# Moving the buffers of a three-layer block within the on-chip memory: weights and residual to the high end, matmul operands and stage pools to the low end

## The chip, the cores and the metric

The kernel runs on one core of a Trainium2 chip, as one launch. The time is the device time of that launch in microseconds, and the median of the runs is what counts. TensorE (PE in the profile) multiplies; its weight loads are shown apart (PEld). VectorE is DVE, ScalarE is ACT, GpSimd is POOL, and SP is SyncE, from whose queue nearly all transfers are issued. All tiles named here lie in SBUF, the on-chip memory, across its 128 partitions; an address below is the byte at which a tile starts in each partition.

## The reference

Three layers over 512 tokens of 1024 features, in float32 (`D_MODEL` 1024, feed-forward width 2816):

```python
# layer 1
attn = dilated_attention(q, k, v)                 # 8 heads, three dilations
sgu = spatial_gating(u, z, ...)                   # gated by a 128 x 128 causal mix
mixed = concat(rmsnorm(attn), rmsnorm(sgu)) @ w_out
h = h + rmsnorm(mixed)
g, up = split(rmsnorm(h) @ w_gate_up)             # 2 x 2816 columns
h = h + rmsnorm((silu(g) * up) @ w_down)
h = h + sigmoid(h @ w_pe_gate + b) * (p @ w_pe_proj)
# layers 2 and 3, each with shift, scale and gate from c
m = stick_breaking_attention(h, w_in, w_out)      # layer 2: 16 heads
m = dsa_attention(h, ...)                         # layer 3: 16 heads, 128 keys of each query picked by an index
h = h + gate * m
u = causal_conv3(rms_norm(h) @ ffn_w_up); h = h + gate * ((silu(u1) * u2) @ ffn_w_down)
```

## The kernel before, in words

Activations lie feature-major, as tiles of 128 features by 512 tokens. Every weight product is made in three passes of `mm3` (L104), since both operands are split into a high and a low part of type fp32r: low weights times high operand, high times high, high times low. One pass is one matmul with a stationary operand of 128 x 128 (or fewer columns) and a moving operand of 128 x 512; the page calls it `out<-moving,stationary` or the other way round, and each has its own weight load.

- **Weights.** `unit` (L87) and `units` (L110) load 128 x 1024 float32 into one of four tiles `raw` by SP's queue, ACT casts each half to `whi` (L98 or L122), and DVE takes the difference as `wlo` (L99 or L123); there are seven of each. As a rule these are the stationary operands. In the token-major products (`tok_steps`, L153) they are the moving ones.
- **Moving operands.** `hh0` to `hh7` and `hl0` to `hl7` hold the high and low parts of a layer's normed input; the up-projections of all feed-forwards read them. `Hh0` to `Hh21` and `Hl0` to `Hl21` hold the 22 feature tiles of a feed-forward's middle, which the down-projections read (`down`, L744). The attention stages' output projections read `mh`, `ml`, `k` or `q` tiles.
- **Stages.** `mixer_a` and `ffn_a` (layer 1), `mixer_sb` and `ffn_conv` (layer 2), `mixer_dsa` and `ffn_conv` (layer 3) follow each other. Each opens a pool of its own and closes it at its end, so that the next stage's pool takes the same addresses. In the feed-forwards PE has one long list of weight products. In the attention stages `attend` (L523) weaves score blocks, transposes and value products with weight products.
- **Placement.** A pool is a stack of tiles in the order of their first use, each start rounded up to a multiple of 32 bytes. Five pools that live throughout (L273 to L276 in `build`, and the residual `X0` to `X7` inside the pool `x`) lie at the bottom, in this order: constants, weights, `x`, small tiles. The stage's pool comes above them.

The starts of the tiles that matmuls read, and what is left when the start is divided by 256, as the built programs have them:

| tile | start before | by 256 | start after | by 256 |
|---|---|---|---|---|
| `raw` (4 tiles of 4096 bytes) | 22784 | 0 | 173920 | 96 |
| `whi`, `wlo` (14 of 2048) | 39168 | 0 | 190304 | 96 |
| `X0` to `X7` | 71936 | 0 | 157536 | 96 |
| `hh`, `hl` (16 of 2048) | 88320 | 0 | 16512 | 128 |
| `Hh`, `Hl` of `ffn_a` | 137888 | 160 | 49280 | 128 |
| `Hh`, `Hl` of `ffn_conv` | 154976 | 96 | 65664 | 128 |
| `mh`, `ml` of `mixer_a` | 137888 | 160 | 57472 | 128 |
| `mh` of `mixer_sb` | 158912 | 192 | 74400 | 160 |
| `q8` to `q15` of `mixer_dsa` | 129696 | 160 | 51328 | 128 |
| `q5`, `q6`, `q7` of `mixer_dsa` | 200704 | 0 | 120288 | 224 |
| `AT`, `v0` of the index in `mixer_dsa` | 162464, 146080 | 160 | 82048, 65664 | 128 |

Tiles of one row follow each other in steps of a multiple of 256, so that a row has one remainder.

Of the kernel before, what the change touches and what calls it, by code (L numbers as in the profile page):

```python
# [8 lines left out]
F32 = mybir.dt.float32  # L9
F32R = mybir.dt.float32r  # L10
# [5 lines left out]
P = 128  # L16
# [14 lines left out]
# Columns of the per-feature constants, eight (or n) columns of 128 features each.  # L31
# [25 lines left out]
class K:  # L57
# [29 lines left out]
    def unit(self, src, widths=(512, 512), eng=None):  # L87
        """One load of consecutive columns, in parts of `widths`: [(hi, lo)]."""
        nc = self.nc
        n, raw = sum(widths), src  # L90
        if src is not self.first:
            raw = self.t(self.wp, [P, UNIT], F32, "raw", bufs=4)
            nc.sync.dma_start(raw[:, :n], src[:, :n])
        out, c = [], 0
        for w in widths:
            hi = self.t(self.wp, [P, 512], F32R, "whi", bufs=7)
            lo = self.t(self.wp, [P, 512], F32R, "wlo", bufs=7)
            nc.scalar.copy(hi[:, :w], raw[:, c:c + w])  # L98
            (eng or nc.vector).tensor_sub(lo[:, :w], raw[:, c:c + w], hi[:, :w].bitcast(F32))  # L99
            out.append((hi, lo))  # L100
            c += w
        return out
# [7 lines left out]
    def units(self, srcs):  # L110
        """Two-part units of several slabs, the first parts of all before the second ones."""
# [15 lines left out]
    def slabs(self, pss, parts, xs, m=P, per=4, ks=None, n=None):  # L127
        """pss[i][m, 512] += sum over k of w_i[k].T @ x[k], k-tile by k-tile for all i together.

        parts[i]: (hi, lo) of `per` k-tiles each, in the order of xs; ks: the k-tiles of this call, of n."""  # L130
# [3 lines left out]
    def slab_steps(self, pss, parts, xs, m=P, per=4, ks=None, n=None):  # L134
        """The products of slabs() one by one, with a pause between two."""
# [12 lines left out]
    def tokmajor(self, pss, srcs, xs):  # L148
        """pss[tb][128 tokens, 512] = x.T @ w, w in units of two k-tiles."""
# [36 lines left out]
    def add_square(self, acc, src, pool=None, tag="acc", eng=None):  # L186
        """acc + src^2; returns the tile that holds the sum."""
# [10 lines left out]
    def rsqrt(self, x, tag="rc", bufs=3, scale=1.0, pool=None):  # L198
        """scale * x^-0.5 of a few columns: a seed from the exponent's bits, then Newton's steps to full precision."""
# [16 lines left out]
    def stats(self, src, ones, out=None):  # L216
        """(mean of squares + eps)^-0.5 as columns [128 tokens, 4] and along the free dimension."""
# [29 lines left out]
    def split(self, src, i, kind="h", pool=None):  # L247
        """The two parts of a moving operand, for k-tile i."""
# [7 lines left out]
    def split_scaled(self, src, col, i, kind="h", pool=None):  # L256
        """Parts of src * col (per feature)."""
# [12 lines left out]
    def build(self):  # L270
        tc, nc, a = self.tc, self.nc, self.a
        with ExitStack() as ctx:
            cp = ctx.enter_context(tc.tile_pool(name="const", bufs=1))  # L273
            self.wp = ctx.enter_context(tc.tile_pool(name="w", bufs=1))
            self.xp = ctx.enter_context(tc.tile_pool(name="x", bufs=1))
            self.sp = ctx.enter_context(tc.tile_pool(name="small", bufs=1))  # L276
# [4 lines left out]
            X = [self.t(self.xp, [P, S], F32, f"X{k}") for k in range(KD)]  # L281
            self.consts = self.t(cp, [P, NCOLS], F32, "consts")
            # what the first products need comes first
# [22 lines left out]
            # modulation: 48 columns a layer; the scales and the deferred shifts of the four norms  # L306
# [28 lines left out]
    # first block: dilated attention and spatial gating  # L335
    def mixer_a(self, X, raw):
# [9 lines left out]
        with ExitStack() as ctx:  # L346
# [4 lines left out]
            # gating: z token-major  # L351
# [12 lines left out]
            # values token-major  # L364
# [29 lines left out]
            # b_c * sum_j w[i, j] + b_s[i], for every channel and row  # L394
# [12 lines left out]
            # u feature-major, the gate and its squares  # L407
# [21 lines left out]
            # attention, by pairs of heads  # L429
# [42 lines left out]
            def filler():  # L472
# [10 lines left out]
                # output projection of the gate's part, with its norm behind it  # L483
# [14 lines left out]
            # then the attention's  # L498
# [24 lines left out]
    def attend(self, pairs, block, av, filler, budget, ahead=0):  # L523
        """Pairs of heads in two stages: the blocks of the next pair's weights, woven with a pair's values and other work.

        block(h, qb): weights of a block of queries; av(i, A): (transposes(kb), products(kb), end());
        filler: other work in steps, budget[i + 1] of them in stage i."""
# [26 lines left out]
    # pairs of 64-dim heads: a head's query parts over each other, against its key's parts twice over each other  # L554
# [26 lines left out]
    def stacked(self, ps, q, k, h, qb, stop=True):  # L581
        """Scores of a block of queries; the first block takes 256 keys, the fewest at full rate."""
# [4 lines left out]
    def post(self, X, M, R, k):  # L587
        """x + the normed branch (its gain is in M)."""
# [3 lines left out]
    def dilated_bias(self, pool, keep):  # L592
        """-(bias + log of how many branches see the pair) without the slope's part, and the distance; 1e30 where none does.

        Column u of row p is at distance d = p + 384 - u; a branch of dilation r sees d when r
        divides it and d <= 128 r (for r = 4 and 16 every d here)."""
# [5 lines left out]
        # d <= 128  # L602
        nc.vector.tensor_scalar(cnt, dist, 128.0, None, op0=ALU.is_le)
        for r in (4, 16):
            # p mod r against u mod r
# [7 lines left out]
        # counts 0..3 to -log(count), 1e30 for none  # L613
# [6 lines left out]
        # beyond the diagonal: none  # L620
# [4 lines left out]
    def softmax(self, pool, sb, nm, L, sign):  # L625
        """exp(sign * sb + nm) / its sum, rows of L."""
        nc = self.nc
        e = self.t(pool, [P, L], F32, f"A{L}", bufs=4)
# [7 lines left out]
    def av(self, pool, A, V, copy):  # L636
        """[2 x 64 dims, 512 queries] of a pair of heads: sum over key blocks of V[kb].T @ A.T, in two steps a key block.

        A[h][qb] is [queries, keys]; V(kb, h) [keys, 64]."""
# [22 lines left out]
    # gated feed-forward, then the per-layer embedding's gate  # L662
    def ffn_a(self, X, M, R):
        tc, nc, a = self.tc, self.nc, self.a
        acc, xs = None, []
        with tc.tile_pool(name="ffn", bufs=1) as fp:
# [11 lines left out]
            for n in range(KF):  # L678
# [7 lines left out]
                g = self.t(fp, [P, S], F32, "g", bufs=2)  # L686
                nc.vector.tensor_mul(g, pg, R)
                nc.scalar.activation(g, g, AF.Silu)
                u = self.t(fp, [P, S], F32, "u", bufs=2)
# [3 lines left out]
            # the embedding's operands  # L693
            es = []
            for k in range(2):
                e = self.t(self.sp, [P, S], F32, "sq", bufs=2)
                nc.scalar.dma_start(e, a["p"][:, k])
                hi = self.t(fp, [P, S], F32R, "g", bufs=2)
                lo = self.t(fp, [P, S], F32R, "u", bufs=2)
# [31 lines left out]
            for n in range(8):  # L731
# [5 lines left out]
                g = self.t(fp, [P, S], F32, "g", bufs=2)  # L737
# [12 lines left out]
    # modulation: silu(c) @ ada_w + ada_b, features on partitions, 128 a step  # L750
# [9 lines left out]
    def dots(self, jobs):  # L760
        """Rows of weights (128 outputs a job) times a row, each loaded a step ahead of its arithmetic."""
# [8 lines left out]
    def ada_steps(self, l):  # L770
# [10 lines left out]
        # all but the gate of the feed-forward, which comes last  # L781
        yield from columns(0, 40)
        for j, norm in enumerate(("norm_mix", "norm_ffn")):
            cn = COLS[f"{norm}{l}"]
            # (scale + 1) * norm
# [4 lines left out]
        # shift @ w for the four slabs that start before their norm is known  # L790
# [16 lines left out]
    def finish(self, X, n, b):  # L807
        """The next norm's operands of feature tile n: its squares, and its parts with the scale but no norm."""
# [11 lines left out]
    def enter(self, X, b, ws):  # L820
        """Four slabs whose norm and shift come behind them, then the normed operand for the others.

        Returns a function that gives slab i in a tile, and the operand."""
# [34 lines left out]
    def project(self, X, src, ms, l, gate, b):  # L858
        """x += gate * (m @ w): (start, rest), the first slabs k-tile by k-tile as their operands come."""
# [10 lines left out]
        def early():  # L870
            # as far as the last but one operand, a fourth slab too
# [19 lines left out]
    # stick-breaking attention  # L891
    def mixer_sb(self, X):
        tc, nc, a = self.tc, self.nc, self.a
        with tc.tile_pool(name="sb", bufs=1) as mp:
# [4 lines left out]
            dmask = self.t(mp, [P, S], F32, "keep", bufs=2)[:, :P]  # L899
            nc.vector.memset(dmask, 0.0)  # L900
            # key >= query: none
# [26 lines left out]
            def block(h, qb):  # L928
# [4 lines left out]
                keep = self.t(mp, [P, S], F32, "keep", bufs=2)  # L933
                nc.scalar.activation(keep[:, :L], ps[:, :L], AF.Sigmoid, scale=-1.0)
                beta = self.t(mp, [P, L], F32, f"A{L}", bufs=4)
                nc.scalar.activation(beta, ps[:, :L], AF.Sigmoid)
                # what is left of the stick before each key, from the query backwards
                # (the last key of a row is never before its query: no weight)
# [5 lines left out]
            def av(i, A):  # L944
                o, tr, mul = self.av(mp, A, lambda kb, h: V[kb][:, (2 * i + h) * 64:(2 * i + h + 1) * 64], None if i == 7 else nc.vector.tensor_copy)
# [30 lines left out]
    # feed-forward with a causal convolution over the tokens  # L976
    def ffn_conv(self, X, l):
        tc, nc, a = self.tc, self.nc, self.a
        with tc.tile_pool(name="ffn", bufs=1) as fp:
            w = a["ffn_w_up"][l]  # L980
            cc = self.t(fp, [P, 4, 44], F32, "conv")
# [4 lines left out]
            for n in range(KF):  # L986
                ys = []
                for j in range(2):
# [7 lines left out]
                    y = self.t(fp, [P, S], F32, "gu"[j], bufs=2)  # L996
# [15 lines left out]
    # sparse attention over the keys that an index picks  # L1012
    def mixer_dsa(self, X):
        tc, nc, a = self.tc, self.nc, self.a
        with ExitStack() as ctx:
            Tw = self.Tw
            mp = ctx.enter_context(tc.tile_pool(name="dsa", bufs=1))
            w = a["dsa_w_in"]
            slab, operand = self.enter(X, 2, [w[i] for i in range(4)])

            # the latent, and the index's queries
# [14 lines left out]
            # index scores and the keys they pick  # L1036
# [24 lines left out]
            def index(qb, h):  # L1061
# [13 lines left out]
                if h == IH - 1:  # L1075
                    # beyond the diagonal: the reference's floor
# [4 lines left out]
            def rounds(n):  # L1081
                # the largest of each row leave it, eight a round, equal ones by lowest index
# [12 lines left out]
            # queries, four heads at a time with their norms  # L1095
# [11 lines left out]
            def norms(h, n=4):  # L1107
                # norms of n heads up to h
# [15 lines left out]
                # the factor of the scores, its negative, and its inverse  # L1124
# [9 lines left out]
            def ahead():  # L1134
                norm = iter(())
                for h in range(5):
# [8 lines left out]
                    if h == 3:  # L1145
                        # the keys: the latent normed, with both gains
# [7 lines left out]
                # values of every head, token-major  # L1154
# [219 lines left out]
```

## Time and profile before

| | |
|---|---|
| median of 3 runs | 1977.55 us (1975.62 to 1977.94) |
| profiled execution, first to last instruction | 1975.4 us, 2.2 us under the median |
| PE busy | 97% of the span, 8610 matmuls |
| DVE, ACT, POOL busy | 67%, 46%, 21% |
| mean granted TensorE clock | 0.986 |

Matmuls overlap: a row's duration is longer than the distance from its start to the next start. What a product costs is that distance, so a run of n products is read as its length divided by n.

### The profile page before, as it was taken

How to read it: one execution, taken by the hardware profiler on the slowest of the kernel's cores; microseconds unless marked ns; L12 is line 12 of the kernel's file. 1: busy time of each engine (PE TensorE's matmuls, PEld its weight loads, DVE VectorE, ACT ScalarE, POOL GpSimd, SP SyncE). 2: the span in 40 equal slices, each digit the busy share in tenths (PEclk: the TensorE clock that was granted, in tenths of full speed). 3: DMA queues.
4: the chain of work that ended last, by engine and by line, in shares of the span. 5: the costliest groups of instructions: out<-in, count | busy, mean ns of one | idle time of the engine just before them, and what ended most of it. 6: DMA issues, size and time to landing. Idle time of an engine off the chain costs nothing.

```text
span 1975.4 us, 24114 instructions
## 1 busy us (share of the span) xinstructions
PE 1918.6 (97%) x8610; PEld 1507.0 (76%) x8610; DVE 1328.2 (67%) x2358; ACT 903.1 (46%) x1672; POOL 416.3 (21%) x376
## 2 busy tenths in 40 slices
PE   7999899999999999999999999999999999999999
PEld 5887678888887777767788888877656678888887
DVE  6686776656355966776988875568967678666421
ACT  4465443323334455554544443336588646444321
POOL 3010421111010402332212110033454241111000
PEclk8999899999999999999999999999999999999999
DMA  5232155555462432222265545522212023223331
GB/s 179 86 91 72 61 186 190 187 183 176 159 213 85 149 117 86 75 65 77 86 213 195 191 154 182 174 81 96 81 59 65 33 77 128 97 95 102 96 106 49
DMA packets 70382, 236.93 MB, mean 120 GB/s; under 512 B 8085, under 2 KB 8677, under 8 KB 70262
## 3 DMA queue, kind: packets, MB, share of 16 engines
q1 hardware_dynamic: 69556, 234.47, 35.6%
q8 instruction: 67, 1.10, 0.2%
q10 hardware_dynamic: 578, 0.85, 0.1%
q14 instruction: 53, 0.43, 0.1%
q0 software_dynamic: 128, 0.08, 0.0%
HBM read 226.87 MB, written 2.21 MB: 116 GB/s over the span
## 4 chain that ended last, share of the span: by engine, by line
PE 84%; DVE 10%; issue 3%; ACT 1%; POOL 1%; DMA 1%; ACTq 0%; DVEq 0%; POOLq 0%; SPq 0%
PE mm L81 50%; PE sc L81 27%; PE po L81 4%; PE tt L84 2%; PE tt L81 1%; DVE isc L1093 1%; DVE m L1092 1%; DVE hl L852 1%; DVE hl L262 1%; DVE wlo L123 1%; DVE wlo L99 1%; DVE Hh L850 1%; DVE X L590 0%; DVE q L850 0%; POOL acc L190 0%
## 5 line engine op out<-in xcount | busy, mean ns | idle before, releaser
L99 DVE TENSOR_TENSOR wlo<-raw,whi 128x512 fp32r<-128x512 f32 (+1 forms) x518 | 392.5, 763 | 241.2 <-ACT whi L98 236.4
L98 ACT CAST whi<-raw 128x512 fp32r<-128x512 f32 (+1 forms) x550 | 328.1, 607 | 424.4 <-PE mm L81 248.9
L81 PE MATMUL mm<-hh,wlo 128*128 128x512 f32 (+1 forms) x1000 | 407.9, 408 | 10.1 <-ACT hh L261 3.5
L81 PE MATMUL mm<-hl,whi 128*128 128x512 f32 x1032 | 402.5, 393 | 0.0
L81 PE MATMUL mm<-hh,whi 128*128 128x512 f32 (+1 forms) x1000 | 392.8, 393 | 0.0
L81 PEld LDWEIGHTS mm<-hh,wlo 128*128 128x128 f32 (+1 forms) x1000 | 189.1, 189 | 78.3 <-issue 30.3
L81 PEld LDWEIGHTS mm<-hl,whi 128*128 128x128 f32 x1032 | 194.8, 189 | 42.7
L81 PEld LDWEIGHTS mm<-hh,whi 128*128 128x128 f32 (+1 forms) x1000 | 189.5, 189 | 36.5 <-issue 0.8
L768 DVE CUSTOM_DVE_ANT_0 ada<-ada,bc 128x1024 f32<-128x1024 f32 x112 | 141.4, 1262 | 62.6 <-DMA ada<-in_ada_w 48.6
L190 POOL TENSOR_TENSOR acc<-acc,sq 128x512 f32<-128x512 f32 x57 | 88.1, 1546 | 427.0 <-ACT sq L195 419.5
L81 PE MATMUL sc<-hh,wlo 128*128 128x512 f32 x416 | 163.1, 392 | 4.8 <-ACT whi L98 3.4
L81 PE MATMUL sc<-hh,whi 128*128 128x512 f32 x416 | 162.8, 391 | 0.0
L81 PE MATMUL sc<-hl,whi 128*128 128x512 f32 x416 | 162.6, 391 | 0.0
L1004 POOL TENSOR_TENSOR g<-g,u 128x512 f32<-128x512 f32 x44 | 69.7, 1584 | 391.7 <-DVE u L1000 359.5
L81 PE MATMUL mm<-Hh,wlo 128*128 128x512 f32 x364 | 144.5, 397 | 2.0 <-DVE wlo L99 2.0
L81 PE MATMUL mm<-Hl,whi 128*128 128x512 f32 x364 | 144.3, 396 | 0.0
L81 PE MATMUL mm<-Hh,whi 128*128 128x512 f32 x364 | 143.6, 395 | 0.0
L252 ACT CAST Hh<-g 128x512 fp32r<-128x512 f32 x66 | 41.0, 622 | 162.7 <-POOL g L691 96.4
L81 PEld LDWEIGHTS sc<-hh,wlo 128*128 128x128 f32 x416 | 78.7, 189 | 21.9 <-ACT whi L98 3.8
L81 PEld LDWEIGHTS sc<-hl,whi 128*128 128x128 f32 x416 | 78.7, 189 | 16.5
L81 PEld LDWEIGHTS sc<-hh,whi 128*128 128x128 f32 x416 | 78.5, 189 | 16.4
L81 PE MATMUL sc<-Hl,whi 128*128 128x512 f32 x220 | 87.4, 397 | 0.0
(371 smaller groups left out, 3411.3 us busy)
## 6 DMA issues: line engine op xcount, KB each, us to landing
ada<-in_ada_w SPq DMA_DIRECT2D x96, 512.0 KB, 3.3
raw<-in_ffn_w_up SPq DMA_DIRECT2D x88, 512.0 KB, 3.3
raw<-in_w_gate_up SPq DMA_DIRECT2D x44, 512.0 KB, 4.1
raw<-in_ffn_w_down SPq DMA_DIRECT2D x32, 512.0 KB, 3.4
raw<-in_sb_w_in SPq DMA_DIRECT2D x24, 512.0 KB, 3.2
raw<-in_dsa_w_in SPq DMA_DIRECT2D x21, 512.0 KB, 3.2
raw<-in_w_in SPq DMA_DIRECT2D x19, 512.0 KB, 3.2
raw<-in_w_down SPq DMA_DIRECT2D x16, 512.0 KB, 3.9
```

What stands on the lines that cost most here:

```text
L81: self.queue(self.nc.tensor.matmul(*args, **kw))
L84: self.queue(self.nc.tensor.transpose(*args))
L98: nc.scalar.copy(hi[:, :w], raw[:, c:c + w])
L99: (eng or nc.vector).tensor_sub(lo[:, :w], raw[:, c:c + w], hi[:, :w].bitcast(F32))
L123: nc.vector.tensor_sub(lo, part, hi.bitcast(F32))
L190: (eng or self.nc.gpsimd).tensor_add(acc, acc, self.square(src))
L252: self.nc.scalar.copy(hi, src)
L262: self.nc.vector.scalar_tensor_tensor(lo, src, col, hi.bitcast(F32), op0=ALU.mult, op1=ALU.subtract)
L768: nc.vector.tensor_tensor_reduce(raw, raw, row, scale=1.0, scalar=0.0, op0=ALU.mult, op1=ALU.add, accum_out=out))
L850: nc.vector.tensor_scalar(f, f, self.A[b][:, k:k + 1], mod[:, sh + k:sh + k + 1], op0=ALU.mult, op1=ALU.add)
L852: nc.vector.tensor_sub(lo, f, hi.bitcast(F32))
L1004: nc.gpsimd.tensor_mul(g, g, u)
```

## The change

All tiles and all instructions stay. What changes is where pools are opened. Pools get a side: constants, weights, a new pool `res` for the residual, and small tiles are stacked from the high end downwards; `x` (now `hh` and `hl` alone) and the stage pools are stacked from the low end upwards. A few tiles of a stage (`g`, `u`, `conv`; `keep` and the attention weights `A`, `AT`) get a second pool that is opened behind the stage's first one, so that the operands of matmuls come lowest. The comments and docstrings are taken out as well.

```diff
-            cp = ctx.enter_context(tc.tile_pool(name="const", bufs=1))
-            self.wp = ctx.enter_context(tc.tile_pool(name="w", bufs=1))
-            self.xp = ctx.enter_context(tc.tile_pool(name="x", bufs=1))
-            self.sp = ctx.enter_context(tc.tile_pool(name="small", bufs=1))
+
+            cp = ctx.enter_context(tc.tile_pool(name="const", bufs=1, side="right"))
+            self.wp = ctx.enter_context(tc.tile_pool(name="w", bufs=1, side="right"))
+            self.rp = ctx.enter_context(tc.tile_pool(name="res", bufs=1, side="right"))
+            self.sp = ctx.enter_context(tc.tile_pool(name="small", bufs=1, side="right"))
+            self.xp = ctx.enter_context(tc.tile_pool(name="x", bufs=1, side="left"))
...
-            X = [self.t(self.xp, [P, S], F32, f"X{k}") for k in range(KD)]
+            X = [self.t(self.rp, [P, S], F32, f"X{k}") for k in range(KD)]
...
-    def softmax(self, pool, sb, nm, L, sign):
+    def softmax(self, pool, sb, nm, L, sign, weights=None):
...
-        e = self.t(pool, [P, L], F32, f"A{L}", bufs=4)
+        e = self.t(weights or pool, [P, L], F32, f"A{L}", bufs=4)
...
-        with tc.tile_pool(name="ffn", bufs=1) as fp:
+        with tc.tile_pool(name="ffn", bufs=1) as fp, tc.tile_pool(name="ffng", bufs=1) as gp:
...
-                g = self.t(fp, [P, S], F32, "g", bufs=2)
+                g = self.t(gp, [P, S], F32, "g", bufs=2)
...
-        with tc.tile_pool(name="sb", bufs=1) as mp:
+        with tc.tile_pool(name="sb", bufs=1) as mp, tc.tile_pool(name="sbw", bufs=1) as ap:
...
-                beta = self.t(mp, [P, L], F32, f"A{L}", bufs=4)
+                beta = self.t(ap, [P, L], F32, f"A{L}", bufs=4)
...
-            cc = self.t(fp, [P, 4, 44], F32, "conv")
+            cc = self.t(gp, [P, 4, 44], F32, "conv")
...
-                    y = self.t(fp, [P, S], F32, "gu"[j], bufs=2)
+                    y = self.t(gp, [P, S], F32, "gu"[j], bufs=2)
...
             mp = ctx.enter_context(tc.tile_pool(name="dsa", bufs=1))
+            ap = ctx.enter_context(tc.tile_pool(name="dsaw", bufs=1))
...
-                return self.softmax(mp, bm, nm, L, r)
+                return self.softmax(mp, bm, nm, L, r, ap)
```

In the built programs PE, DVE, ACT and POOL have the same instructions in the same order. SP's queue differs at two places, the entries of the two `ffn_conv` stages, where the load of the convolution's taps (`conv`) stands. This is SP's queue at the first of them, ahead of the change (`raw` are weight tiles, `in_ffn_w_up` the up-projection's weights):

```order
L116 DMA raw_8032<-in_ffn_w_up 128x1024
L116 DMA raw_8034<-in_ffn_w_up 128x1024
L116 DMA raw_8036<-in_ffn_w_up 128x1024
L116 DMA raw_8038<-in_ffn_w_up 128x1024
L93 DMA raw_8281<-in_ffn_w_up 128x1024
L93 DMA raw_8320<-in_ffn_w_up 128x1024
L982 DMA conv_8026<-in_conv 128x176
```

And SP's queue at the same place with the change:

```order
L116 DMA raw_8046<-in_ffn_w_up 128x1024
L984 DMA conv_8040<-in_conv 128x176
L116 DMA raw_8048<-in_ffn_w_up 128x1024
L116 DMA raw_8050<-in_ffn_w_up 128x1024
L116 DMA raw_8052<-in_ffn_w_up 128x1024
L93 DMA raw_8295<-in_ffn_w_up 128x1024
L93 DMA raw_8334<-in_ffn_w_up 128x1024
```

The taps' load moves from behind six weight loads to behind the first. It writes where an attention weight tile (`A512`, `AT`) of the stage before lay, so it waits for PE's last reads of those; before it wrote where small tiles of that stage lay.

## Rows read from the trace of the kernel before

**Rows 1.** The page's head: span, and busy time of each engine.

```profile
span 1975.4 us, 24114 instructions
PE 1918.6 (97%) x8610; PEld 1507.0 (76%) x8610; DVE 1328.2 (67%) x2358; ACT 903.1 (46%) x1672; POOL 416.3 (21%) x376
```

**Rows 2.** The page's chain that ended last, by engine.

```profile
PE 84%; DVE 10%; issue 3%; ACT 1%; POOL 1%; DMA 1%; ACTq 0%; DVEq 0%; POOLq 0%; SPq 0%
```

**Rows 3.** Chain in order of time: start us, us, what.

```profile
542.48 46.40 PE mm L81 x198
...
910.00 23.78 PE mm L81 x102
...
1157.22 16.32 PE mm L81 x72
...
1194.50 46.20 PE mm L81 x198
```

**Rows 4.** Stretches of two feed-forwards: busy us (count), PEclk, DMA share, GB/s.

```profile
970.00:1170.00 200.00, 200.00 (x884) 165.59 (x884) 171.85 (x248) 94.28 (x155) 36.00 (x20) 1.00 0.55 191
1180.00:1300.00 120.00, 120.00 (x516) 96.52 (x515) 61.69 (x92) 36.86 (x63) 9.29 (x7) 1.00 0.49 160
```

**Rows 5.** Timeline of PE, output projection of mixer_dsa, operand tiles q4 to q9.

```profile
1586.43 0.64 PE L81 MATMUL mm<-q,whi 128*128 128x512 f32 x2
...
1587.13 0.61 PE L81 MATMUL mm<-q,whi 128*128 128x512 f32 x2
...
1587.82 0.62 PE L81 MATMUL mm<-q,whi 128*128 128x512 f32 x2
```

**Rows 6.** Timeline of PE, value products of mixer_dsa (stationary q14, q15).

```profile
1388.49 0.40 PE L81 MATMUL mm<-wlo,q 128*128 128x512 f32 x1
...
1393.40 0.39 PE L81 MATMUL mm<-wlo,q 128*128 128x512 f32 x1
```

**Rows 7.** Chain in order of time, index of mixer_dsa: AT pairs between trios.

```profile
1349.75 0.46 PE sc L81 x2
1350.21 0.69 PE mm L81 x3
...
1354.36 0.46 PE sc L81 x2
```

**Rows 8.** The page's costliest groups, matmuls that read hh and hl.

```profile
L81 PE MATMUL mm<-hh,wlo 128*128 128x512 f32 (+1 forms) x1000 | 407.9, 408 | 10.1 <-ACT hh L261 3.5
L81 PE MATMUL mm<-hl,whi 128*128 128x512 f32 x1032 | 402.5, 393 | 0.0
...
L81 PE MATMUL sc<-hh,wlo 128*128 128x512 f32 x416 | 163.1, 392 | 4.8 <-ACT whi L98 3.4
```

**Rows 9.** Groups of PE: products with the feed-forward's middle; products with weights moving.

```profile
L81 PE MATMUL mm<-Hh,wlo 128*128 128x512 f32 x364 | 144.5, 397 | 2.0 <-DVE wlo L99 2.0
...
L81 PE MATMUL sc<-Hl,whi 128*128 128x512 f32 x220 | 87.4, 397 | 0.0
...
L81 PE MATMUL mm<-whi,hl 128*128 128x512 f32 x80 | 34.1, 426 | 9.1 <-DVE hl L262 7.2 <-DVE sq L835 1.9
```

**Rows 10.** Groups of DVE and ACT, one shape: aligned tiles, then Hh and Hl.

```profile
L99 DVE TENSOR_TENSOR wlo<-raw,whi 128x512 fp32r<-128x512 f32 x492 | 381.4, 780 | 208.4 <-ACT whi L98 203.6 <-PE mm L81 4.1
...
L253 DVE TENSOR_TENSOR Hl<-g,Hh 128x512 fp32r<-128x512 f32 x66 | 46.7, 707 | 40.1 <-ACT Hh L252 34.8
...
L98 ACT CAST whi<-raw 128x512 fp32r<-128x512 f32 x524 | 317.7, 617 | 375.6 <-PE mm L81 219.0 <-PE sc L81 118.6 <-PE po L81 22.4
L252 ACT CAST Hh<-g 128x512 fp32r<-128x512 f32 x66 | 41.0, 622 | 162.7 <-POOL g L691 96.4 <-POOL g L1004 66.2
```

**Rows 11.** Timeline of SP's queue at the first entry of ffn_conv.

```profile
915.58 5.04 SPq L116 DMA_DIRECT2D raw<-in_ffn_w_up  x3
...
932.48 0.33 SPq L982 DMA_DIRECT2D conv<-in_conv  x1
```

**Rows 12.** Timeline of PE, last reads of attention weights in mixer_sb.

```profile
905.17 0.44 PE L81 MATMUL po<-AT,v 128*64 128x128 f32 x4
```

More of the change, by code (lines that the diff above doesn't have):

```diff
@@ L685, in ffn_a @@
                 ps = ps[2:]
-                g = self.t(fp, [P, S], F32, "g", bufs=2)
+                g = self.t(gp, [P, S], F32, "g", bufs=2)
                 nc.vector.tensor_mul(g, pg, R)
                 nc.scalar.activation(g, g, AF.Silu)
-                u = self.t(fp, [P, S], F32, "u", bufs=2)
+                u = self.t(gp, [P, S], F32, "u", bufs=2)
                 nc.vector.tensor_mul(u, pu, R)
@@ L697, in ffn_a @@
                 nc.scalar.dma_start(e, a["p"][:, k])
-                hi = self.t(fp, [P, S], F32R, "g", bufs=2)
-                lo = self.t(fp, [P, S], F32R, "u", bufs=2)
+                hi = self.t(gp, [P, S], F32R, "g", bufs=2)
+                lo = self.t(gp, [P, S], F32R, "u", bufs=2)
                 nc.scalar.copy(hi, e)
@@ L736, in ffn_a @@
                     self.slabs(ps, [self.unit(a["w_pe_gate"][n])], xs)
-                g = self.t(fp, [P, S], F32, "g", bufs=2)
+                g = self.t(gp, [P, S], F32, "g", bufs=2)
                 nc.scalar.activation(g, ps.pop(0), AF.Sigmoid, bias=self.col("b_pe_gate", n))
@@ L898, in mixer_sb @@
             nc.vector.tensor_copy(identb, self.ident)
-            dmask = self.t(mp, [P, S], F32, "keep", bufs=2)[:, :P]
+            dmask = self.t(ap, [P, S], F32, "keep", bufs=2)[:, :P]
             nc.vector.memset(dmask, 0.0)
@@ L932, in block @@
                 self.matmul(ps[:, L - P:L], identb, dmaskb, start=False, stop=True)
-                keep = self.t(mp, [P, S], F32, "keep", bufs=2)
+                keep = self.t(ap, [P, S], F32, "keep", bufs=2)
                 nc.scalar.activation(keep[:, :L], ps[:, :L], AF.Sigmoid, scale=-1.0)
-                beta = self.t(mp, [P, L], F32, f"A{L}", bufs=4)
+                beta = self.t(ap, [P, L], F32, f"A{L}", bufs=4)
                 nc.scalar.activation(beta, ps[:, :L], AF.Sigmoid)
@@ L944, in av @@
             def av(i, A):
-                o, tr, mul = self.av(mp, A, lambda kb, h: V[kb][:, (2 * i + h) * 64:(2 * i + h + 1) * 64], None if i == 7 else nc.vector.tensor_copy)
+                o, tr, mul = self.av(ap, A, lambda kb, h: V[kb][:, (2 * i + h) * 64:(2 * i + h + 1) * 64], None if i == 7 else nc.vector.tensor_copy)
                 def end():
@@ L978, in ffn_conv @@
         tc, nc, a = self.tc, self.nc, self.a
-        with tc.tile_pool(name="ffn", bufs=1) as fp:
+        with tc.tile_pool(name="ffn", bufs=1) as fp, tc.tile_pool(name="ffng", bufs=1) as gp:
             w = a["ffn_w_up"][l]
-            cc = self.t(fp, [P, 4, 44], F32, "conv")
+            cc = self.t(gp, [P, 4, 44], F32, "conv")
             nc.sync.dma_start(cc, a["conv"][l])
```

## The prediction

> **What bounds the kernel now.** I read the page's head first: PE is busy 97% of 1975.4 us, DVE 67% [rows 1]. The chain that ended last says the same in another way, 84% of it is PE [rows 2]. So the kernel costs what its matmuls cost, one behind the other, and a change that moves no instruction counts if it changes that price. The reader is to look at the price next. The chain in order of time has long runs of weight products without any gap, all 128 x 512, at full clock in the stretches of [rows 4]. An up-projection's run has 72 in 16.32 us, 226.7 ns each. A down-projection's has 198 in 46.20 us, 233.3 ns each; the one in layer 1 has 198 in 46.40, 234.3 ns; the output projection of `mixer_sb` has 102 in 23.78, 233.1 ns [rows 3]. The windows agree: 884 matmuls in 200 us against 516 in 120 [rows 4]. PE waits for nobody in either. The same instruction on the same shapes has two prices, 6.67 ns apart.
>
> What differs is where the operands lie. The cheap run reads weights and `hh`, `hl`, and all of these start at a multiple of 256 bytes. The dear runs read the same weights with `Hh`, `Hl`, `mh`, `ml`, whose starts leave 96, 160 or 192. The dear tiles also lie higher, above 129,000 bytes, so height is a second reading. One place parts the two: `q5`, `q6` and `q7` lie above 200,000 and start at multiples of 256, between neighbours that leave 224 and 160. The pair that reads `q6` and `q7` takes 0.61 us, the others 0.62 to 0.64 [rows 5], the shortest of its sweep. It is a small difference, but it is on the side of alignment. The price of a remainder of 192 equals that of 96 [rows 3], so 64 bytes are not enough; whether 128 are, no tile here tells.
>
> Does the stationary operand count too? In the value products the moving operand is `whi` or `wlo` (remainder 0), and the stationary ones are `q14` and `q15` (remainder 160). From the first row to the last are 21 products in 4.91 us, 233.8 ns each [rows 6]. So an unaligned weight load costs as much as an unaligned moving operand. And both at once? In the index, two products with `AT` moving and `v0` stationary (160 both) stand between three aligned ones. From 1349.75 to 1354.36 are four such groups of five, 1.1525 us each [rows 7]; at 226.7 ns five would take 1.133, so 19 ns are shared by the two: more than 2 x 6.67, less than 2 x 13.3.
>
> **The change part by part.** *Weights, from remainder 0 to 96.* They are the stationary operand of nearly all products. The products that are cheap now are those of `hh` and `hl` with weights, three passes each: 3 x 1000 in `mm`, 3 x 416 in `sc` [rows 8], and 3 x 80 in which weights move [rows 9], some 4,500 in all, with a few hundred in smaller groups beside them. At 6.67 ns each that is +30 us. Of these, some 36 slabs of 24 products, 860, are woven into the attention stages, where a trio of aligned products takes 0.69 us, 230 ns each, because of its neighbours [rows 7]; half of the price is paid there already: -2.9 us. Nothing hides the rest: in the long runs PE has no gap [rows 4].
>
> *Moving operands, to remainder 128 (160 in `mixer_sb`).* The 364 and 220 trios of `Hh` and `Hl` [rows 9] pay 6.67 ns now. If 128 is good enough, they lose that and gain the weights' price: nothing changes but the 1.0 ns by which layer 1's are dearer (528 products, -0.5 us). The same holds for the `mh` and `q` products. If 128 isn't good enough, every product has both operands unaligned; by [rows 7] the second one costs from nothing (the excess belongs to the changes between aligned and unaligned) to 6.67 ns again. I take nothing, because the cleanest runs with one unaligned operand pay the one price wherever it comes from, and keep the other end for the range.
>
> *Other engines.* DVE's and ACT's operands get unaligned as well. For one shape DVE takes 780 ns on aligned tiles and 707 on `Hl`, `Hh`, ACT 617 and 622 [rows 10]: no price that shows, and DVE, at 171.85 of 200 us in its fullest stretch [rows 4], gets more room from a slower PE. Zero. If there were a price of 10%, DVE would still fit (189 of 206 us).
>
> *The taps' load.* It now stands ahead of three weight loads on SP's queue and waits for the last reads of `AT`. Those end by 905.6 us [rows 12], ten before the loads behind it were issued, at 915.58 [rows 11], since they wait for their `raw` tiles anyhow. Zero; without that cover it would hold back the loads of four slabs. At its old place the load took 0.33 us, and nobody waited for it.
>
> The sum: +30.1 - 2.9 - 0.5 = +27 us on 1975.4. The runs' median is 2.2 us above that execution; I add the change to the median: 1977.55 + 27 = 2004.5 us, +1.4%.
>
> **The rivals.** *Both operands pay.* If 128 leaves a moving operand unaligned and prices add, then the cheap 4,500 pay 10 to 13.3 ns and the dear ones (3 x 364 + 3 x 220 and some 650 of the attention's projections, 2,400) 3.3 to 6.7 ns more: +45 + 8 - 4 = +49 at the lower, +60 + 16 - 4 = +72 at the upper end, 2027 to 2050 us. For it speaks the 19 ns of [rows 7], against it that these products stand between changes of operand.
>
> *The weights' place is free.* This is the case that ends faster: what looks like the stationary operand's price in [rows 6] is something of that stage, and only the moving operand counts, by height or by a boundary of 128. Then the dear 2,400 become cheap: -2,400 x 6.67 = -16 us, 1961.5. It decides from the point at which the weight load costs under 2.3 ns a product (6,900 such products against 16 us). Against it are the 21 products in a row at 233.8 ns, with aligned weights moving, which have no other source of delay; for it, that they are all from one place of 5 us. If the weights' place is free but 128 is not enough, all products are dear again and the time is that of the forecast.
>
> *Nothing happens.* The two prices follow the stage, not the tiles (what DVE and the transfers do meanwhile): 1977.5 us. Against it: in the cheap run transfers and DVE are busier than in the dear one (0.55 and 86% against 0.49 and 51%) [rows 4], so that the load would have to act the wrong way round. The Trainium skill ("SBUF — State Buffer", Who interferes with whom) is on this rival's side: TensorE has two read ports of its own, one for the moving operand and one for weight loads, and waits for no one, and the page gives no price to the place of an operand. By it the sum would be zero. The trace doesn't agree: the two prices of [rows 3] stand where only operands differ, so I leave this rival a small chance.
>
> **How the numbers follow.** The forecast has 0.70, both operands pay 0.17, free weights 0.08, nothing 0.05. The forecast's own range is 1997 to 2012: the price from 5 to 8 ns on 4,500 products. The range for 8 in 10 reaches from there to the middle of the dearer case: 1993 to 2040. From no change a measurement of this kernel tells about 0.2%, 4 us. Faster 0.08, within it 0.05, slower 0.87.
>
> **What would show it.** In the profile after, the chain's runs of 72 in the up-projections must take 16.8 us, those of 198 still 46.2 and not 48; PE's gaps and waits stay as they are, and DVE's and ACT's durations too. If the runs of 72 stay at 16.32 and those of 198 fall to 44.9, free weights it was. 17.3 and 47.5 or more say that both pay. PE's wait at the entries of `ffn_conv`, on `wlo`, would show that the taps' load holds up weights. The prediction is wrong if alignment isn't what the two prices follow; all of it hangs on that reading and on the 21 products of [rows 6].

## The result and the profile after

The changed kernel takes 1995.67 us, median of 4 runs (1992.68 to 1995.80); the kernel before, run beside it, 1977.68 (1975.62 to 1977.94). The ratio is 1.0093, with a 95% interval from 1.0078 to 1.0108: 18 us slower, where 27 were forecast. The time lies in the wide range of the prediction (1993 to 2040) and 1.3 us under the narrow one (1997 to 2012). The head of the page of the kernel after, which answers to [rows 1]:

```profile
span 1993.9 us, 24111 instructions
PE 1940.0 (97%) x8610; PEld 1502.5 (75%) x8610; DVE 1327.7 (67%) x2358; ACT 904.1 (45%) x1672; POOL 415.7 (21%) x376
```

The other engines are busy as long as before. PE has the same 8610 matmuls and 21 us more of busy time. The chain of the kernel after in order of time (start us, us, what), with the pieces of [rows 3]:

```profile
551.47 46.21 PE mm L81 x198
...
918.45 23.36 PE mm L81 x102
...
973.42 16.80 PE mm L81 x72
...
1169.42 16.80 PE mm L81 x72
...
1207.33 46.20 PE mm L81 x198
```

The runs of 72 went from 16.32 to 16.80 us, 226.7 to 233.3 ns a product. The runs of 198 stayed (layer 1's 46.40 became 46.21). One row was not foreseen: `mixer_sb`'s output projection, 102 products, fell from 23.78 to 23.36, 229.0 ns a product, though its operands leave 160 and 96, neither of them a multiple of 256.

Windows of the kernel after, over stretches as long as those of [rows 4] (columns as there), and its groups of DVE that answer to [rows 10]:

```profile
976.00:1176.00 200.00, 200.00 (x858) 160.66 (x858) 169.36 (x243) 92.89 (x155) 37.20 (x20) 1.00 0.55 187
1190.00:1310.00 120.00, 120.00 (x516) 96.34 (x515) 61.23 (x91) 37.27 (x64) 9.32 (x7) 1.00 0.53 165
```

```profile
L99 DVE TENSOR_TENSOR wlo<-raw,whi 128x512 fp32r<-128x512 f32 x492 | 380.1, 778 | 215.2 <-ACT whi L98 212.8 <-PE sc L81 1.9
...
L253 DVE TENSOR_TENSOR Hl<-g,Hh 128x512 fp32r<-128x512 f32 x66 | 46.7, 707 | 38.4 <-ACT Hh L252 33.1
```

200 us of an up-projection now hold 858 products in place of 884, and 120 us of a down-projection 516 as before, at full clock and without a gap. DVE takes the same time on tiles with other remainders (780 and 707 ns before), and so does ACT (617 and 621 ns, 617 and 622 before).

### The profile page after: what moved, and what is told of

Same layout as the page of the kernel before. It is cut to its first block, busy times and chain, and to the rows that moved or that the text cites. A ratio compares the mean times of both kernels' runs of the same rounds, so it can differ in the third digit from the quotient of the medians.

```text
span 1993.9 us, 24111 instructions
## 1 busy us (share of the span) xinstructions
PE 1940.0 (97%) x8610; PEld 1502.5 (75%) x8610; DVE 1327.7 (67%) x2358; ACT 904.1 (45%) x1672; POOL 415.7 (21%) x376
## 4 chain that ended last, share of the span: by engine, by line
PE 86%; DVE 9%; issue 2%; ACT 1%; POOL 1%; DMA 0%; SPq 0%; ACTq 0%; DVEq 0%; POOLq 0%
PE mm L81 51%; PE sc L81 27%; PE po L81 4%; PE tt L84 2%; PE tt L81 1%; DVE isc L1096 1%; DVE m L1095 1%; DVE hl L262 1%; DVE hl L854 1%; DVE wlo L123 1%; DVE Hh L852 1%; DVE wlo L99 0%; DVE X L592 0%; DVE v L1033 0%; POOL acc L190 0%
## 5 line engine op out<-in xcount | busy, mean ns | idle before, releaser
L81 PE MATMUL mm<-hh,whi 128*128 128x512 f32 (+1 forms) x1000 | 396.8, 397 | 0.0
L81 PEld LDWEIGHTS sc<-hl,whi 128*128 128x128 f32 x416 | 78.4, 188 | 19.2
L81 PE MATMUL sc<-Hh,wlo 128*128 128x512 f32 x220 | 87.0, 395 | 0.0
```

Of the source, the lines that this page charges most:

```text
L81: self.queue(self.nc.tensor.matmul(*args, **kw))
```

## The experiments

The three kernels that measure products by themselves ran once each.

**The disputed price by itself.** The body of the kernel is replaced by trios whose operands are slices of larger tiles, so that moving operand and weights start at any multiple of 32 bytes:

```diff
+                for m in range(8):
+                    for s in range(8):
...
+                        xh, xl = (t[:, 8 * m_:8 * m_ + 512] for t in x)
+                        for k in range(16):
+                            c = 8 * s_ + k % 4 * P
+                            self.mm3(ps, w[0][:, c:c + P], w[1][:, c:c + P], xh, xl, k == 0, k == 15)
```

> This kernel leaves the whole computation out and writes x to the output; it measures the disputed price by itself. Trios of the kernel's weight products (128 x 128 stationary, 128 x 512 moving) run without a wait, 48 for each pair of remainders: the moving operand's start leaves 0, 32, ... 224 by 256 bytes, the weights' start too, first from tiles at the low end of the memory (lowM..W..), then at the high end (highM..W..). My theory (a remainder of either operand costs one price, 6.67 ns, and the second nothing): 226.7 ns (48 in 10.88 us) where both are 0, 233.3 (11.20) everywhere else, low and high alike. Both operands pay: 226.7, 233.3 where one is unaligned, 236 to 240 where both are. The weights' place is free: 226.7 in the whole row of moving remainder 0. Height: low and high differ. The traces of before and after already hold one pair that fits none of these, moving 160 with weights 96 at about 229 ns; if the price is a matter of both remainders together, pairs with both unaligned spread between 226.7 and 234, and (160, 96) is one of the cheaper ones. If quiet surroundings take the price away (nothing else runs here), all 64 are equal.

The chain in order of time of this kernel; a piece's name has the place, the moving operand's remainder (M) and the weights' (W). In the built program the high tiles themselves start 224 past a multiple of 256, so that both remainders of a high piece are 224 more than its name says (by 256), and their difference is as named:

```profile
399.74 11.20 PE lowM128W96x L81 x48
410.93 10.89 PE lowM128W128x L81 x48
...
455.45 11.24 PE lowM160W0x L81 x48
...
489.05 11.00 PE lowM160W96x L81 x48
...
711.75 10.88 PE lowM224W224x L81 x48
722.63 10.88 PE highM0W0x L81 x48
...
822.94 10.88 PE highM32W32x L81 x48
```

Both operands at 224, or both at 128, are as cheap as both at 0 (`highM32W32`, by its name's 32 and the 224); (128, 96), the pair of the changed kernel, is dear. All pieces but the first, in which PE starts, fall in order by one number, the moving operand's start less the weights', by 256 bytes (16 pieces to a difference, 15 to 0):

| difference | shortest to longest piece, us | ns a product |
|---|---|---|
| 0 | 10.88 to 10.92 | 226.9 |
| 64 | 10.98 to 11.00 | 229.0 |
| 160 | 11.23 to 11.25 | 234.1 |
| 32, 96, 128, 192, 224 | 11.16 to 11.21 | 233.2 |

So my theory fell, and the additive one with it: where all products of a run have one pair of remainders, the price isn't set by the remainder of either operand but by the difference between the two. Low and high tiles agree within 0.04 us, so height plays no part. The table also explains the odd row of the profile after: (160, 96) has difference 64.

**Four layouts of the whole kernel.** They ran on one chip, five or six times each, beside 11 runs of the kernel before (median 1975.97 us). The first two are the changed kernel with one line more, which moves the weights to 128, or with 24 in place of 56 to 0:

```diff
+            self.t(cp, [P, 56], F32, "pad")
             X = [self.t(self.rp, [P, S], F32, f"X{k}") for k in range(KD)]
```

> The changed kernel with 224 bytes of padding ahead of the weight pool, so that the weights leave 128 as hh, hl, Hh and Hl do; neither operand is aligned. Theory D (the price follows the difference of the two remainders, as in the table): 7,025 of the 7,272 products of 512 columns have difference 0, so every product costs what the cheap ones cost before: before's 1977.5 less 6.67 ns for its some 2,400 dear products, about 1962, and the chain's runs of 72 in 16.32 us, of 198 in 44.9. Theory E (a remainder of either operand costs the price once, that of my prediction): as the changed kernel, 1995.7, runs of 72 in 16.80 and of 198 in 46.2.

> The changed kernel with 96 bytes of padding ahead of the weight pool: the weights start at multiples of 256 again, the moving operands keep their 128. This undoes the part of the change that my prediction put the whole price on. Theory D: the difference is 128 in place of 32, the same price, 1996 (+1 at most for mixer_sb's output projection, whose difference goes from 64 to 160). Theory E: 1996 as well if 128 counts as a remainder; if weights are what counts and a moving 128 is free, 1962.

The other two are the kernel before, with the weights alone moved to 96, and with all operands at multiples of 256 (here without the padding of single small tiles inside the stages):

```diff
+            self.t(self.wp, [P, 24], F32, "pad")
+            self.t(self.xp, [P, 40], F32, "pad")
             X = [self.t(self.xp, [P, S], F32, f"X{k}") for k in range(KD)]
```

```diff
+            self.t(self.sp, [P, 24], F32, "pad")
             if self.ffn_a(X, M, R) == "stop":
...
+            self.t(fp, [P, 16], F32, "pad")
             slab, operand = self.enter(X, 2 * l + 1, [w[i] for i in range(4)])
```

> The kernel before with the weights alone moved by 96 bytes (padding of 96 ahead of them and 160 behind, so that all else keeps its place): one part of the change alone. Theory D: hh and hl with weights get difference 160 (234.3 ns, +7.6 on the some 2,850 products that pay in full: +21.7), Hh and Hl of both ffn_conv get 0 (-6.67 x 1,056 = -7.0), those of ffn_a and a few operands of the mixers 64 (-5.4 x 720 = -3.9): 1988; runs of 72 in 16.87 us, of 198 in 44.9 in ffn_conv and 45.3 in ffn_a. Theory E: the cheap products pay once, the dear ones pay already: as the changed kernel, 1996; runs of 72 in 16.80, of 198 still 46.2.

> The kernel before with padding (96 bytes ahead of the stage pools, some more behind the small tiles in them) so that every operand of the products of 512 columns starts at a multiple of 256, at the old ends of the memory. Both D and E: about 1962, runs of 198 in 44.9 us. It tells whether the ends of the memory cost anything by themselves: by D it equals the run with weights and moving operands at 128 on the new ends (within 3 us); if the place matters beyond the remainders, they differ.

| layout | median, us | ratio to before, 95% interval |
|---|---|---|
| after, weights at 128 (difference 0) | 1962.05 | 0.9931 (0.9919 to 0.9942) |
| after, weights at 0 (128) | 1992.31 | 1.0078 (1.0062 to 1.0095) |
| before, weights at 96 (160, 0, 64) | 1991.58 | 1.0080 (1.0067 to 1.0093) |
| before, all at 0 (difference 0) | 1962.51 | 0.9929 (0.9917 to 0.9941) |

The chain of the changed kernel with weights at 128, which came out at the time that the difference gave and 33.6 us below the old theory's:

```profile
310.59 16.32 PE mm L81 x72
...
1186.38 44.94 PE mm L81 x198
```

With weights at 0:

```profile
1001.31 16.80 PE mm L81 x72
...
1207.22 46.01 PE mm L81 x198
```

The kernel before with weights at 96:

```profile
318.00 16.87 PE mm L81 x72
...
553.46 45.34 PE mm L81 x198
...
1209.77 44.91 PE mm L81 x198
```

And with all at 0:

```profile
311.09 16.32 PE mm L81 x72
...
1186.30 44.91 PE mm L81 x198
```

Two unaligned operands at the same remainder are as fast as two aligned ones, and aligning the weights alone, which my prediction had charged with the whole price, gives next to nothing back. The run with weights at 96 parts the theories best: the same padding made the up-projections dearer (16.87) and both kinds of down-projections cheaper (45.34, 44.91), within 0.02 us of what the table gives. Its sum, forecast at +10.5, was +15.6. By the starts of the same instruction in both traces, 2.7 us of it arise by 236 us and 1.3 between 720 and 935, in the first two mixers, whose cheap products my sum had left out. The two layouts of difference 0 lie at opposite ends of the memory and differ by 0.5 us: the ends cost nothing by themselves.

These two layouts also answer [rows 7]. The chain of the changed kernel with weights at 128, at the same instructions:

```profile
1338.54 0.45 PE sc L81 x2
1338.99 0.68 PE mm L81 x3
...
1343.07 0.45 PE sc L81 x2
```

The same 20 products take 4.53 us here and in the layout with all at 0, 226.7 ns each, and took 4.61 in the kernel before. In all three each product's own two operands agree; but before, `AT` and `v0` left 160 and the trios between them 0, and in these two layouts all leave the same. So a product is dear beside products of another remainder even where its own difference is 0.

**Whose weights.** PE loads the weights of the next product beside the current one's stream: in the trace of the kernel before, a product with `hh` and `wlo` starts at 1099.93 us, the weight load of the next one at 1099.94, and that next product at 1100.16. Pieces whose remainders alternate should tell which pairing counts.

```diff
+            piece("own0next128", [(0, 0), (128, 128)])
+            piece("own128next0", [(0, 128), (128, 0)])
...
+            for d in (0, 4, 8, 16, 28, 32, 48, 64, 80, 96):
+                piece(f"M{d}W0", [(d, 0)])
```

> As the table, the whole computation is left out and x is written to the output; 96 products a piece, none waits. Open is which two operands the price belongs to: a product's moving operand and its own weights, or its moving operand and the weights that are loaded beside it for the next product. The pieces take their remainders in turn. Theory own: own0next128, own0next160 and own0next64 cost what own0 does (21.76 us, 226.7 ns), own128next0, own160next0 and own64next0 cost 22.4 or so. Theory next (weights are read for the next product while this one's operand streams, and the two reads meet): the other way round, 22.4 for the first three (22.0 for 64) and 21.76 for the last three. The pieces M4W0 to M96W0 look for the step at which the difference begins to count: by the tiles' places, multiples of 32, nothing smaller was seen; if any shift costs, 4 bytes do. Pieces with 256 and 384 columns tell whether the price is per product (6.67 ns at any width) or per column (3.3 and 5.0). The bf pieces ask the same of bfloat16 operands.

The chain of this kernel:

```profile
31.25 21.77 PE own0x L81 x96
...
75.34 21.92 PE own0next128x L81 x96
97.26 22.08 PE own128next0x L81 x96
119.33 22.45 PE own0next160x L81 x96
141.79 22.08 PE own160next0x L81 x96
...
230.27 22.72 PE M4W0x L81 x96
...
297.62 21.76 PE M28W0x L81 x96
319.38 22.40 PE M32W0x L81 x96
...
364.18 22.40 PE M64W0x L81 x96
...
475.85 11.51 PE cols256M0W0x L81 x96
487.36 11.31 PE cols256M32W0x L81 x96
...
521.25 16.64 PE cols384M0W0x L81 x96
537.90 16.64 PE cols384M32W0x L81 x96
...
608.56 20.72 PE bfM32W0x L81 x96
```

This did not settle it: with 128 and 64 the products' own pairing looks cheaper (for 64, 22.24 against 22.40), with 160 the next one's, and none reaches the 21.77 of difference 0. Every product of the pieces `own0next` has difference 0, and all three pieces are dearer, so its own two operands alone don't decide. Two more things are clear. Of the kinds that were run, only 512 columns of fp32r are cheapest at difference 0: with 384 columns all four differences take 16.64 us, with bfloat16 all five 20.72 to 20.74, and with 256 columns 0 is the dearest (11.51, the others 11.27 to 11.31). And below 32 bytes it doesn't go by size, since 4 bytes cost more than any other and 28 nothing. Here, where high and low parts alternate together, 64 costs the full price, while in trios it costs a third.

**Trios between short products.** The layouts left open why the cheap products outside of the up-projections had paid so little.

```diff
+                    piece(f"T{trios}S{short}C{cols}D{d}", d, trios, short, cols)
```

> Again the whole computation is left out and x is written to the output. Open is why the some 1,600 cheap products outside of the up-projections, most of them trios woven between the short products of the attention stages, paid next to nothing in the changed kernel. Each piece has 32 times so many trios (T1, T2, T4) with the moving operand at remainder D and the weights at 0, and after each so many short products (S0, S1, S3) of C columns, whose operands both leave 160; nothing waits. Theory neighbours (a trio among products of other shapes costs the same at any difference): the pieces T1S1 and T1S3 differ by less than 0.2 us between D0 and D32. Theory cover (the price is there, and waits for other engines hide it in the kernel): each trio of D32 costs 3 x 6.67 ns more, 0.64 us a piece with T1, 1.28 with T2, 2.56 with T4, as in the piece without short products (T1S0).

The chain of this kernel (96 of the products of T1 are trios, 192 of T2, 384 of T4):

```profile
31.47 21.76 PE T1S0C256D0x L81 x96
53.23 22.40 PE T1S0C256D32x L81 x96
...
142.41 26.10 PE T1S1C256D0x L81 x128
168.50 26.03 PE T1S1C256D32x L81 x128
...
439.66 48.00 PE T2S1C256D0x L81 x224
487.66 48.00 PE T2S1C256D32x L81 x224
...
680.53 55.67 PE T2S3C256D0x L81 x288
736.20 56.30 PE T2S3C256D32x L81 x288
...
959.76 99.23 PE T4S3C256D0x L81 x480
1058.99 100.90 PE T4S3C256D32x L81 x480
```

A trio alone between short products costs the same at difference 0 and 32. Two in a row pay nothing of 1.28 us with one short product behind them and 0.63 with three, four pay 1.67 of 2.56. Nothing waits here, so no cover of another engine is at work.

The two are equal because both are dear. By the starts in the trace, the three products of a lone trio (T1S1C256) take 698 ns at difference 0 and 693 at 32, where the unbroken pieces take 680 and 700. Of twelve in a row at difference 0 (T4S3) the inner ones take 226 to 227 ns each, the first and the last 236. So it is the cheap price that needs an unbroken run of one remainder: the trios here leave 0 and the short products 160, as in the index before.

## Why the prediction came out as it did

**Right in the main.** The trace's two prices were read rightly, and so was which runs would become dear: 16.80 us for 72, 46.2 for 198. The ranges were less well worked out: with the -2.9 taken off, 8 ns on 4,500 products ends at 2010 and not 2012, and the wide range's lower end of 1993, which the measured time needs, is derived nowhere. No engine but PE changed. The taps' load cost nothing: at the entry of `ffn_conv` PE never waits for `wlo`, and 3.0 us for `whi` (3.4 before).

**The step that was mis-sized is the first term, 4,500 products at 6.67 ns.** 3,168 of them are the up-projections' (three stages of 44 slabs of 24), and these paid: in the second stage the pieces of 72 follow each other from 973.42 to 1169.42 in steps of 28.00 us, where before a step was 27.20, 0.80 us on 120 products. By the starts of the same instruction in both traces the three up-projections together cost 19 us, of 21 at the full price. The others paid some 2.8 us, 1.0 in `mixer_a`, 1.2 in `mixer_sb` and 0.6 in `mixer_dsa`, where the forecast had 6 (8.9 for 1,300 products, less 2.9; there are some 1,600). So the first term and what was taken off it, 27.2 us, measured 22. I had seen that a trio in the attention stages takes 230 ns at difference 0, and taken half of the price off for 860 products; the trios between short products showed that a lone trio has nothing more to lose, since it is already dear. The kernel itself shows it too: the 20 products of the index take 4.61 us before and 4.64 after. Over one woven stretch of `mixer_sb`, with 268 products of `hh` and `hl`, windows of the changed kernel and of that with weights at 128, the same 616 matmuls:

```profile
765.00:880.00 115.00, 115.00 (x616) 81.60 (x615) 89.68 (x120) 62.80 (x142) 37.10 (x46) 1.00 0.29 83
```

```profile
748.92:863.82 114.90, 114.90 (x616) 81.64 (x615) 89.64 (x120) 62.79 (x142) 37.10 (x46) 1.00 0.28 83
```

0.1 us, where 268 full prices are 1.8. The rest of the difference came from places that got cheaper: layer 1's down-projection (-0.5, as forecast), `mixer_sb`'s projection (-0.6, of which 0.4 on the 102 products of its long run), and half-clock stretches (-2.4 in all). The granted clock of the kernel before falls to half at the first `ffn_conv`'s entry (window 958 to 966), that of the kernel after not at that place (964 to 972). The same holds in `mixer_dsa` (0.79 from 1428 to 1436 before, 1.00 from 1440 to 1448 after), and a stretch at 701 us became half as long. In their place the kernel after has one more in the first up-projection (262 to 268). By the starts of the instructions in them, a stretch of 3.4 us costs some 1.5 us.

```profile
958.00:966.00 8.00, 6.50 (x22) 5.24 (x23) 7.87 (x14) 5.57 (x10) 0.00 (x0) 0.79 0.39 131
```

```profile
964.00:972.00 8.00, 4.99 (x22) 3.75 (x21) 8.00 (x15) 4.75 (x9) 0.00 (x0) 1.00 0.20 66
262.00:268.00 6.00, 4.98 (x19) 4.32 (x20) 4.35 (x8) 1.52 (x3) 1.89 (x2) 0.72 0.65 204
```

These add up to 19.2 + 2.8 - 3.5, the 18.5 us of the profiled executions.

**Wrong in its reason.** "Start at a multiple of 256" was the wrong rule, and it gave the right prices by luck: before, all weights left 0, so that the moving operand's remainder was also the difference; after, nearly all products have a difference of 32, one of the many that cost the same. It failed where I could have tested it, at the 19 ns of [rows 7]. I read them as something between one price and two for `AT` and `v0`, both at 160, beside three products at 226.7 ns; but by the starts all five take about 230.7 ns, the difference of each is 0, and the excess goes where all remainders agree (4.53 us above). So it belongs to the passage from products at 0 to products at 160 and back. That one product's operand meets another's weights there is argued and not shown. The rule also hid the better layout: 224 bytes of padding make the changed kernel 0.7% faster than the one before.

**The rivals.** Both operands pay, free weights and height fell with the table. "Nothing happens" fell with the 34 us of span between two layouts that differ by 224 bytes of padding (1993.9 and 1959.9). The Trainium skill ("SBUF — State Buffer", Who interferes with whom) has TensorE's two reads on ports of their own and gives a start no price; the table differs, for these products, and the measurement decides.

## What to carry to other kernels

Where fp32r products of 512 columns run one behind the other, bring the moving operands and the weights of all of them to the same remainder by 256 bytes, whichever it is; a padding tile ahead of one pool does it. Read the price of a product from the distance between starts in a long run, and don't charge it to products that stand between others of another remainder: they pay already. When a rule from a trace names one operand, vary the other as well: a constant can hide in it.

## What was not expected of the hardware

- In unbroken trios one and the same matmul takes 226.9, 229.0, 233.2 or 234.1 ns, as its two operands' starts stand to each other by 256 bytes. At 384 columns it takes 173.3 ns at all four differences that were run, and at 256 columns difference 0 is the dearest (11.51 us for 96, the others 11.27 to 11.31).
- A product whose own difference is 0 takes 230.7 ns where its neighbours have another remainder, and 226.7 where all have the same.
- A difference of 64 costs a third of the price in trios (229.0 ns) and all of it where high and low parts of both operands alternate from product to product (22.40 us for 96).
- Bfloat16 operands of the same shape take 215.8 to 216.0 ns at any of five differences.
- Half-clock stretches of the trace move with the layout: the mean granted clock is 0.986 before and 0.988 after. Why stretches fall away or appear stays open.
